# The first shift and scale columns loaded in two pieces, the token root of the latent stream summed on TensorE

## The chip, the cores and the metric

The kernel runs on one core of a Trainium2 chip. The metric is the device time of one execution in microseconds (us). Several executions are timed, and one execution is also recorded by the hardware profiler; its trace gives the rows below.

## What is computed

One layer of a diffusion backbone, in float32, for 512 latent tokens (`x`) and 256 context tokens (`ctx`) of width 2048. The part that matters here is its head:

```python
mod = c_act @ w_mod + b_mod            # 2048 x 12288; sh1 and sc1 are its first 2 x 2048 columns
h  = rmsnorm(x,   g_norm1) * (1 + sc1)  + sh1
hc = rmsnorm(ctx, g_norm1) * (1 + csc1) + csh1
z  = h @ w_in                          # the same for hc; split into heads: q, k (128 each), v (256), ...
```

`rmsnorm` divides each token by the root of the mean square over its 2048 channels. After that come scans over four GLA and four mLSTM heads, an output projection, a gated residual, a second norm, a convolutional MLP and a last norm.

## The kernel before

Activations lie transposed: a channel tile is 128 channels on the partitions by 512 tokens (`xl[k]`, k from 0 to 15, 256 KB each) or by 256 context tokens (`xc[k]`, loaded in pairs). Every large matmul is done as three passes on operands split into a rounded part and a remainder (`hTh`, `hTl` for the stream, `hi_h`, `lo_h` for the weights): ScalarE casts the first, VectorE subtracts to get the second (`split`, lines 89 and 90).

`project_first` is the stage that the diff touches. It projects head 0 (weights `w0`, sums in six PSUM banks, `project_chunk`) and head 1 (weights `w1`, `early_group`, whose partial sums are evicted to SBUF) while the shift and scale columns are still being made. It walks over eight pairs of channel tiles (`kp`). For every pair it needs, in this order:

- the shift (region 0) and scale (region 1) columns of the two tiles. `mod_load` fetches 4 pieces of 512 KB of `w_mod1` for 256 columns of one region, `mod_rows` multiplies them on TensorE with the activated conditions (16 products of 128x32 by 128x256), ScalarE copies the rows out, and `mod_cols` turns them into columns with two small products, from which VectorE makes `scol` or `shcol`;
- `modulate`: a multiplication by the token root, a multiply and add with scale and shift, then the split;
- six groups (`g`): q, k, two pairs of token blocks of v, and two blocks of context tokens.

The token root (`stream_rstd`) is made by squares on ScalarE, a running sum `tot` on VectorE over 16 tiles, a product with a matrix of ones that lays the sum on all partitions, and six operations on 128x512 tiles. The context's root is made in the same way from 8 tiles.

In `project_first` all matmuls are pinned: TensorE runs them in the order of the program text. `tc.high_priority()` moves other engines' work ahead in the order that the scheduler writes out. `tc.issue_after(ins)` queues what its block issues on the engine of `ins` (VectorE here) behind `ins`. All loads go through the queue of SyncE, in program order as the trace shows them; a load into a pool's buffer waits there until the buffer's last reader is done. The pool `mraw` holds four pieces, `wraw` four (weights, and every fourth piece of `w_mod1`), `whi` and `wlo` two each; PSUM has two buffers for the small work (`psb`).

Of the kernel before, what the change touches and what calls it, by code (L numbers as in the profile page):

```python
# [11 lines left out]
F32 = mybir.dt.float32  # L12
F32R = mybir.dt.float32r
U8 = mybir.dt.uint8
AF = mybir.ActivationFunctionType
# [3 lines left out]
P = 128  # L19
D = 2048  # L20
KT = D // P
KP = KT // 2
T = 512
TJ = T // P
# [19 lines left out]
C_SA = C_SEG + T  # L44
C_ONE = C_SA + 32
# [24 lines left out]
def block_kernel(ctx: ExitStack, tc: tile.TileContext, a: dict, out: bass.AP):  # L70
    nc = tc.nc
    V, S, G, PE = nc.vector, nc.scalar, nc.gpsimd, nc.tensor

    def pool(stack, name, bufs=1, space=None, waits="pool"):
        if space is None:
            return stack.enter_context(tc.tile_pool(name=name, bufs=bufs, reuse_waits=waits))
        return stack.enter_context(tc.tile_pool(name=name, bufs=bufs, space=space))
# [128 lines left out]
    def mod_load(region, n):  # L206

        raws = []
        for q in range(4):
            raws.append((wraw if q == 3 else mraw).tile([P, 4, 256], F32, name=f"raw_m{region}_{n}_{q}", tag="raw"))  # L210
            nc.sync.dma_start(raws[q], a["w_mod1"][8 * region + n, q])
        return raws

    def mod_rows(region, n, raws):

        bank = psb(f"ps_m{region}_{n}")
        ps = bank[:, 0:256]
# [4 lines left out]
        rows = tmp.tile([P, 256], F32, name=f"rows_m{region}_{n}", tag="rows")  # L222
        with tc.high_priority():
            S.copy(rows, ps)
        return bank, rows

    def mod_cols(region, n, bank, rows):

        pc = bank[:, 256:260].rearrange("p (b c) -> p b c", c=2)
        for b in range(2):  # L230
            mm(pc[:, b, :], rows[:, P * b : P * b + P], cc(C_SA, 2), start=True, stop=True)
        with tc.high_priority():
            for b in range(2):
                k = 2 * n + b
# [49 lines left out]
        return accp.tile([P, T], F32, name=f"sum{i}_{name}", tag=f"sum{i}")  # L284


    def project_chunk(kp, wh, wl, o, g, first=0, last=KT - 1):

        ks = list(enumerate((2 * kp, 2 * kp + 1)))
        if g < 2:  # L290
            c = slice(P * g, P * g + P)
            for kk, k in ks:
                mm3(o, wh[:, kk, c], wl[:, kk, c], hx[0][k], hx[1][k], k == first, k == last)
        elif g < 4:
            for b in range(2):
                js = slice(P * (2 * g - 4 + b), P * (2 * g - 3 + b))
                for kk, k in ks:
                    mm3(o[:, b, :], hx[0][k][:, js], hx[1][k][:, js], wh[:, kk, 256:], wl[:, kk, 256:],
                        k == first and b == 0, k == last, skip_group_check=True)
        else:  # L300
            js = slice(P * (g - 4), P * (g - 3))
            for kk, k in ks:
                mm3(o, hc[0][k][:, js], hc[1][k][:, js], wh[:, kk, P:], wl[:, kk, P:], k == first, k == last)
# [27 lines left out]
    def project_first():  # L331

        banks = [acc(f"a0_{g}", BANKS[g]) for g in range(6)]
        sums = [None] * 4 + [accp.tile([P, DK + DV], F32, name=f"e0_{4 + j}", tag=f"sum{j}") for j in range(CJ)]
        stream_rstd(xl, rl, "l", T)
        for r in (1, 0):
            mod_cols(r, 0, *mod_rows(r, 0, mod_load(r, 0)))
        w1, w0 = (load_split(a["w_heads"][h, 0], f"h{h}_0") for h in (1, 0))
        for j in range(KT // 2):
            nc.sync.dma_start(xcp[j], a["ctxT"][j])  # L340
        raws = {r: mod_load(r, 1) for r in (1, 0)}
        with tc.high_priority():
            ins = modulate(0, "x")
        for g in range(4):
            early_group(0, g, w1, sums)
        project_chunk(0, *w0, banks[0], 0)
        rows = mod_rows(1, 1, raws[1])
        project_chunk(0, *w0, banks[1], 1)
        mod_cols(1, 1, *rows)
        with tc.high_priority(), tc.issue_after(ins):  # L350
            stream_rstd([x.rearrange("p a b -> p (a b)") for x in xcp], rc, "c", TC)
            ins = modulate(0, "c")
        for g in range(2, 4):
            project_chunk(0, *w0, banks[g], g)
        rows = mod_rows(0, 1, raws[0])
        early_group(0, 4, w1, sums)
        mod_cols(0, 1, *rows)
        early_group(0, 5, w1, sums)
        with tc.issue_after(ins):
            modulate(1, "xc")  # L360
        w1 = load_split(a["w_heads"][1, 1], f"h1_1")
        for r in (1, 0):
            raws[r] = mod_load(r, 2)
        nc.sync.dma_start(cst[:, 0:C_SA], a["consts"][:, 0:C_SA])
# [3 lines left out]
        mod_cols(1, 2, *rows)  # L368
        for kp in range(1, KP):
            for g in range(6):  # L370
                if g == 5 and kp + 1 < KP:
                    rows = mod_rows(0, kp + 1, raws[0])
                ins = early_group(kp, g, w1, sums)
                if g == 2:
                    with tc.issue_after(ins):
                        w0 = load_split(a["w_heads"][0, kp], f"h0_{kp}")
                    if kp + 2 < KP:
                        raws[1] = mod_load(1, kp + 2)
            if kp + 1 < KP:
                mod_cols(0, kp + 1, *rows)  # L380
                with tc.issue_after(ins):
                    modulate(kp + 1, "xc")
            for g in range(6):
                if g == 3 and kp + 2 < KP:
                    rows = mod_rows(1, kp + 2, raws[1])
                project_chunk(kp, *w0, banks[g], g)
                if g == 2 and kp + 1 < KP:
                    w1 = load_split(a["w_heads"][1, kp + 1], f"h1_{kp + 1}")
                    if kp + 2 < KP:
                        raws[0] = mod_load(0, kp + 2)  # L390
                if g == 3 and kp + 2 < KP:
                    mod_cols(1, kp + 2, *rows)
        return banks, sums


# [31 lines left out]

    nc.sync.dma_start(cv, a["cvec"])
    nc.sync.dma_start(cst[:, C_SA:], a["consts"][:, C_SA:])
    nc.sync.dma_start(cols, a["cols"])  # L430
    xl = [ytile(k, f"xl{k}") for k in range(KT)]
    xcp = [actp.tile([P, 2, TC], F32, name=f"xc{j}", tag=f"al{KT // 2 + j}") for j in range(KT // 2)]
# [14 lines left out]
    def stream_rstd(xs, o, name, n):  # L447

        tot = xp.tile([P, T], F32, name=f"sq_{name}", tag="sqs")
        for k, x in enumerate(xs):  # L450
            sq = tot if k == 0 else tmp.tile([P, T], F32, name=f"sq_{name}{k}", tag="sq")
# [6 lines left out]
        var = tmp.tile([P, n], F32, name=f"var_{name}", tag="sq")  # L458
        scr = tmp.tile([P, n], F32, name=f"scr_{name}", tag="sq")
        mean_eps(var, ps, D)  # L460
        rsqrt(var, scr, o)

    rl, rc = rstd[:, 0:T], rstd[:, T:]

    def modulate(n, streams):
        for k in (2 * n, 2 * n + 1):
            if "x" in streams:
                mul(xl[k], xl[k], rl)
            if "c" in streams:
                mul(xc[k], xc[k], rc)  # L470
        for k in (2 * n, 2 * n + 1):
# [656 lines left out]
def arrange(x, c, ctx, c_ctx, w_mod, b_mod, g_norm1, g_norm2, w_in, gla_w_lr, gla_b_lr, mlstm_b_gate,  # L1128
# [10 lines left out]
    r = {}  # L1139
# [7 lines left out]
    r["w_mod1"] = w_mod[0][:, : 2 * D].reshape(4, 4, P, 16, 256).transpose(3, 0, 2, 1, 4)  # L1147
# [42 lines left out]
```

## Time and profile before

| | |
|---|---|
| median of 3 timed runs | 2608.57 us (2608.11 to 2610.57) |
| profiled execution | 2605.73 us, of it the traced span 2604.0 us |
| TensorE busy in the span | 2540.7 us (98%) |
| VectorE, ScalarE, GpSimd busy | 1354.1, 873.3, 230.2 us |
| moved by DMA | 321.39 MB, 123 GB/s over the span |

In the rows below PE is TensorE's matmuls, PEld its weight loads, DVE VectorE, ACT ScalarE, SPq SyncE's queue, which issues the loads. A float32 product of `mm` appears as two MATMUL records. PEclk is the clock granted to TensorE, 1.00 for 2.4 GHz and 0.50 for 1.2 GHz.

### The profile page before, as it was taken

Reading aid. Unit: us, or ns where it says so; the run is one execution under the profiler, and the core shown is the slowest. Engines: PE = TensorE matmul, PEld = TensorE weight load, DVE = VectorE, ACT = ScalarE, POOL = GpSimd, SP = SyncE. Lnnn points to the kernel's source line nnn. Section 1 sums busy time; section 2 is a strip of 40 time slices with the busy share of each in tenths; the row PEclk is TensorE's granted clock in tenths of the full one; section 3 lists DMA queues with packets and bytes.
Section 4 is the critical chain, followed back from the end, with each engine's and each line's share of the span. In section 5 each row is a group of like instructions: output and inputs, shape, how many; then the busy total and the mean of one; then the engine's idle time right before and its main releaser. Section 6 shows DMA issues by size and latency. Waiting matters only on the chain.

```text
span 2604.0 us, 31932 instructions
## 1 busy us (share of the span) xinstructions
PE 2540.7 (98%) x12866; PEld 2132.3 (82%) x12866; DVE 1354.1 (52%) x1969; ACT 873.3 (34%) x1289; POOL 230.2 (9%) x183
## 2 busy tenths in 40 slices
PE   5999999999999999999999999999999999999998
PEld 4887888888897878878878888888888888888887
DVE  6566765553344455448576336533653365336534
ACT  4224543332324344334443123312331233123332
POOL 0000000111212223210331000000000000000001
PEclk9999999999999999999999999999999999999999
DMA  8851112222333576642654322333333223322333
GB/s 312 291 194 42 33 41 74 73 79 84 122 122 122 191 227 220 201 140 85 213 182 146 97 97 98 97 97 97 97 96 97 96 95 96 98 96 90 100 97 101
DMA packets 96349, 321.39 MB, mean 123 GB/s; under 512 B 10884, under 2 KB 15304, under 8 KB 96200
## 3 DMA queue, kind: packets, MB, share of 16 engines
q1 hardware_dynamic: 96200, 319.34, 37.4%
q8 instruction: 101, 1.65, 0.3%
q14 instruction: 48, 0.39, 0.0%
HBM read 315.10 MB, written 4.19 MB: 123 GB/s over the span
## 4 chain that ended last, share of the span: by engine, by line
PE 87%; DVE 4%; DMA 4%; ACT 2%; issue 2%; POOL 1%; SPq 0%; POOLq 0%; ACTq 0%; DVEq 0%
PE a L95 18%; PE dn L95 17%; PE ug L95 17%; PE uv L95 17%; PE wo L95 6%; DMA raw_m<-in_w_mod 4%; PE ga L95 4%; PE po L95 3%; PE ps_m L95 1%; PE sl L95 1%; DVE cv L1037 1%; PE dl L95 1%; POOL sum_m L257 1%; PE cst L95 0%; PE s L95 0%
## 5 line engine op out<-in xcount | busy, mean ns | idle before, releaser
L95 PE MATMUL ug<-h2h,hi_ug 128*128 128x512 f32 x688 | 269.0, 392 | 1.6 <-ACT h2h L996 1.6
L95 PE MATMUL uv<-h2h,lo_uv 128*128 128x512 f32 x688 | 267.9, 389 | 1.5 <-DVE lo_uv L90 1.5
L95 PE MATMUL ug<-h2h,lo_ug 128*128 128x512 f32 x688 | 268.7, 390 | 0.1
L95 PE MATMUL ug<-h2l,hi_ug 128*128 128x512 f32 x688 | 268.4, 390 | 0.0
L95 PE MATMUL uv<-h2h,hi_uv 128*128 128x512 f32 x688 | 267.9, 389 | 0.5 <-ACT hi_uv L89 0.5
L95 PE MATMUL uv<-h2l,hi_uv 128*128 128x512 f32 x688 | 267.7, 389 | 0.0
L95 PE MATMUL dn<-gh,hi_d 128*128 128x512 f32 x644 | 250.5, 389 | 0.0
L95 PE MATMUL dn<-gl,hi_d 128*128 128x512 f32 x644 | 250.5, 389 | 0.0
L95 PE MATMUL dn<-gh,lo_d 128*128 128x512 f32 x644 | 250.5, 389 | 0.0
L1037 DVE SCALAR_TENSOR_TENSOR cv<-pad,cwt,cv 128x512 f32<-128x512 f32 x344 | 242.3, 759 | 10.6 <-ACT cv L1035 9.1
L90 DVE TENSOR_TENSOR lo_ug<-raw_ug,hi_ug 128x1024 fp32r<-128x1024 f32 (+1 forms) x88 | 107.4, 1220 | 238.7 <-ACT hi_ug L89 238.6
L257 POOL TENSOR_TENSOR sum_m<-sum_m,raw_m 128x512 f32<-128x512 f32 x112 | 177.8, 1588 | 577.1 <-ACT raw_m L256 360.3
L90 DVE TENSOR_TENSOR lo_uv<-raw_uv,hi_uv 128x1024 fp32r<-128x1024 f32 (+1 forms) x88 | 105.4, 1198 | 182.1 <-ACT hi_uv L89 181.6
L90 DVE TENSOR_TENSOR lo_d<-raw_d,hi_d 128x1024 fp32r<-128x1024 f32 x82 | 98.7, 1203 | 165.5 <-ACT hi_d L89 164.6
L89 ACT CAST hi_ug<-raw_ug 128x1024 fp32r<-128x1024 f32 (+1 forms) x88 | 90.8, 1032 | 262.4 <-PE ug L95 194.7
L89 ACT CAST hi_d<-raw_d 128x1024 fp32r<-128x1024 f32 x82 | 85.1, 1037 | 278.7 <-PE dn L95 224.4
L255 DVE SCALAR_TENSOR_TENSOR sum_m<-raw_m,csil,sum_m 128x512 f32<-128x512 f32 x112 | 95.0, 849 | 158.4 <-DMA raw_m<-in_w_mod 158.0
L89 ACT CAST hi_uv<-raw_uv 128x1024 fp32r<-128x1024 f32 (+1 forms) x88 | 90.9, 1033 | 250.5 <-PE uv L95 181.1
L95 PEld LDWEIGHTS ug<-h2h,hi_ug 128*128 128x128 f32 x688 | 129.8, 189 | 28.7 <-ACT h2h L996 1.9
L95 PEld LDWEIGHTS uv<-h2h,lo_uv 128*128 128x128 f32 x688 | 129.1, 188 | 29.3 <-DVE lo_uv L90 2.4
L95 PEld LDWEIGHTS ug<-h2h,lo_ug 128*128 128x128 f32 x688 | 129.6, 188 | 28.2 <-DVE lo_ug L90 1.0
L95 PEld LDWEIGHTS ug<-h2l,hi_ug 128*128 128x128 f32 x688 | 129.7, 189 | 27.0
(302 smaller groups left out, 5218.5 us busy)
## 6 DMA issues: line engine op xcount, KB each, us to landing
raw_m<-in_w_mod SPq DMA_DIRECT2D x192, 512.0 KB, 4.3
raw_ug<-in_w_up SPq DMA_DIRECT2D x80, 512.0 KB, 3.4
raw_uv<-in_w_up SPq DMA_DIRECT2D x80, 512.0 KB, 3.3
raw_d<-in_w_down SPq DMA_DIRECT2D x79, 512.0 KB, 3.5
raw_h<-in_w_heads SPq DMA_DIRECT2D x64, 512.0 KB, 3.4
raw_ga<-in_w_gates SPq DMA_DIRECT2D x32, 512.0 KB, 4.3
raw_wo<-in_w_out SPq DMA_DIRECT2D x32, 512.0 KB, 4.3
xl<-in_xT SPq DMA_DIRECT2D x16, 256.0 KB, 5.1
```

Source lines behind the costliest of these rows:

```text
L89: S.copy(hi, x)
L90: return V.tensor_tensor(out=lo, in0=x, in1=hi.bitcast(F32), op=ALU.subtract).ins
L95: ins = PE.matmul(*args, **kw)
L255: V.scalar_tensor_tensor(out=dv, in0=raw[:, 0, :], scalar=ce, in1=dv, op0=ALU.mult, op1=ALU.add)
L257: G.tensor_tensor(out=po, in0=po, in1=raw[:, 1, :], op=ALU.add)
L1037: V.scalar_tensor_tensor(out=t3, in0=src, scalar=w, in1=t3, op0=ALU.mult, op1=ALU.add)
```

## The change

The first two pieces of shift and scale columns (256 columns of each region) are loaded as two times 128 columns from an own array `w_mod0` (two loads of 512 KB for each piece). The products and columns are made for one channel tile at a time, and head 0 begins with channel tile 0 alone (`only=0`), then tile 1. Head 1's first groups follow behind them. The latent stream's squares are added in pairs on VectorE and summed over channels on TensorE into four columns (tokens on partitions); the root is worked out on 128x4 tiles, and four products with the identity lay it on all partitions again (`rb`). The first two tiles are multiplied by `rb` before their columns are there (`scaled`); ScalarE copies `rb` to `rl` for the others. The identity's 64 KB are loaded ahead of `xl` instead of later with the other constants. The weights `w0` are loaded before the first pieces, `w1` between them. `mraw` has six buffers.

```diff
-        stream_rstd(xl, rl, "l", T)
-        for r in (1, 0):
-            mod_cols(r, 0, *mod_rows(r, 0, mod_load(r, 0)))
-        w1, w0 = (load_split(a["w_heads"][h, 0], f"h{h}_0") for h in (1, 0))
+        ss = psb("ss_l", (P, TJ))
+        for k in range(0, KT, 2):
+            sqs = [tmp.tile([P, T], F32, name=f"sq_l{k + i}", tag=f"sq{i}") for i in range(2)]
+            for i in range(2):
+                S.activation(sqs[i], xl[k + i], AF.Square)
+            if k < KT - 2:
+                add(sqs[0], sqs[0], sqs[1])
+                del sqs[1]
+            for i, sq in enumerate(sqs):
+                for j in range(TJ):
+                    mm(ss[:, j : j + 1], sq[:, P * j : P * j + P], cst[:, C_ONE : C_ONE + 1], ...)
+        w0 = load_split(a["w_heads"][0, 0], "h0_0")
+        halves = [{r: mod_load_half(r, 0) for r in (1, 0)}]
+        w1 = load_split(a["w_heads"][1, 0], "h1_0")
+        halves.append({r: mod_load_half(r, 1) for r in (1, 0)})
         for j in range(KT // 2):
             nc.sync.dma_start(xcp[j], a["ctxT"][j])
         raws = {r: mod_load(r, 1) for r in (1, 0)}
+        rows = mod_rows(1, 0, halves[0][1], P)
+        var, scr, r = (xp.tile([P, TJ], F32, name=f"{n}_l") for n in ("var", "scr", "rs"))
         with tc.high_priority():
-            ins = modulate(0, "x")
+            mean_eps(var, ss, D)
+            rsqrt(var, scr, r)
+        rb = psb("rb_l")
+        for j in range(TJ):
+            mm(rb[:, P * j : P * j + P], r[:, j : j + 1].to_broadcast([P, P]), ident, start=True, stop=True)
+        mod_cols(1, 0, *rows, 1)
+        rows = mod_rows(0, 0, halves[0][0], P)
+        mod_cols(0, 0, *rows, 1)
+        with tc.high_priority():
+            for k in range(2):
+                mul(xl[k], xl[k], rb)
+            S.copy(rl, rb)
+            ins = modulate((0,), "x", True)
         for g in range(4):
-            early_group(0, g, w1, sums)
-        project_chunk(0, *w0, banks[0], 0)
-        rows = mod_rows(1, 1, raws[1])
-        project_chunk(0, *w0, banks[1], 1)
-        mod_cols(1, 1, *rows)
+            project_chunk(0, *w0, banks[g], g, only=0)
+        for r in (1, 0):
+            mod_cols(r, 1, *mod_rows(r, "0b", halves[1][r], P), 1)
+        with tc.high_priority():
+            ins = modulate((1,), "x", True)
+        for g in range(4):
+            project_chunk(0, *w0, banks[g], g, only=1)
         with tc.high_priority(), tc.issue_after(ins):
             stream_rstd([x.rearrange("p a b -> p (a b)") for x in xcp], rc, "c", TC)
-            ins = modulate(0, "c")
-        for g in range(2, 4):
-            project_chunk(0, *w0, banks[g], g)
+            ins = modulate((0, 1), "c")
+        for g in range(3):
+            early_group(0, g, w1, sums)
+        rows = mod_rows(1, 1, raws[1])
+        early_group(0, 3, w1, sums)
+        mod_cols(1, 2, *rows)
+        early_group(0, 4, w1, sums)
         rows = mod_rows(0, 1, raws[0])
-        early_group(0, 4, w1, sums)
-        mod_cols(0, 1, *rows)
         early_group(0, 5, w1, sums)
+        mod_cols(0, 2, *rows)
         with tc.issue_after(ins):
-            modulate(1, "xc")
+            modulate((2, 3), "xc")
...
-    mraw = pool(st_0, "mraw", 4)
+    mraw = pool(st_0, "mraw", 6)
```

Behind this, in both kernels: `load_split` of head 1's second pair, `mod_load` for the third pair, `project_chunk(4)`, `mod_rows(1, 2)`, `project_chunk(5)`, `mod_cols`, and then the loop over `kp` from 1 to 7, which is the same but for the numbering of the columns.

## Rows read from the trace of the kernel before

**Rows 1.** The page: busy time, share of the span and instructions of each engine.
```profile
PE 2540.7 (98%) x12866; PEld 2132.3 (82%) x12866; DVE 1354.1 (52%) x1969; ACT 873.3 (34%) x1289; POOL 230.2 (9%) x183
```

**Rows 2.** Windows of 10 us: busy time by engine, PEclk, DMA share, GB/s.
```profile
0.00:10.00 10.00, 0.00 (x0) 0.00 (x0) 4.95 (x12) 5.27 (x8) 0.20 (x4) 1.00 0.71 228
10.00:20.00 10.00, 1.21 (x2) 0.50 (x2) 7.62 (x11) 6.30 (x10) 0.00 (x0) 1.00 1.04 411
20.00:30.00 10.00, 5.96 (x62) 2.20 (x60) 4.78 (x9) 1.63 (x3) 0.00 (x0) 0.97 0.75 270
...
50.00:60.00 10.00, 9.64 (x97) 7.18 (x95) 8.61 (x21) 4.78 (x11) 0.00 (x0) 1.00 0.88 320
60.00:70.00 10.00, 9.50 (x72) 8.15 (x76) 5.66 (x12) 0.94 (x4) 0.00 (x0) 1.00 0.89 323
...
80.00:90.00 10.00, 10.00 (x65) 9.27 (x63) 5.47 (x9) 2.10 (x4) 0.00 (x0) 1.00 0.91 352
```

**Rows 3.** The chain of waits from 0 to 150 us: start, us, what.
```profile
18.79 2.07 PE ss_l L95 x2
...
23.17 6.79 DMA raw_m<-in_w_mod
...
35.75 8.85 PE a L95 x41
...
62.75 6.79 PE a L95 x42
69.55 1.86 PE ps_m L95 x32
71.41 1.26 PE a L95 x6
72.67 0.34 PE ps_m L95 x4
73.00 4.30 PE a L95 x24
```

**Rows 4.** Timeline, 2 to 35 us: start, us, instruction, what ended the idle time before.
```profile
2.18 8.57 SPq L435 DMA_DIRECT2D xl<-in_xT  x16
...
8.48 10.25 DVE L86 TENSOR_TENSOR sq_l<-sq_l,sq_l 128x512 f32<-128x512 f32 x13 [0.62 <-ACT sq_l L452]
...
20.79 2.79 PE L95 MATMUL ps_m<-raw_m,cact 128*32 128x256 f32 x32
...
30.01 1.08 PE L95 MATMUL ps_m<-raw_m,cact 128*32 128x256 f32 x8 [0.60 <-DMA raw_m<-in_w_mod]
...
32.70 0.34 DVE L239 TENSOR_SCALAR shcol<-ps_m,cols 128x2 f32<-128x2 f32 x2 [5.51 <-PE ps_m L95]
...
34.21 0.80 PE L95 MATMUL a<-hTh,hi_h 128*128 128x512 f32 x1 [1.62 <-ACT hTh L89]
```

**Rows 5.** Waits of the load queue from 13 to 15 us: us, times, longest.
```profile
SPq L211 <- DMA xl<-in_xT: 0.6, 2, 0.3
```

**Rows 6.** Timeline of the second norm's token root, which is made in column form.
```profile
1163.36 2.39 PE L968 MATMUL ps_rms<-cst,sqsq 128*128 128x1 f32 x20 [0.76 <-ACT sqsq L956]
...
1165.79 0.16 DVE L154 TENSOR_SCALAR rs_rms<-ps_rms 128x4 f32<-128x4 f32 x1 [1.76 <-PE ps_rms L968]
...
1167.36 2.05 PE L975 MATMUL rb_rms<-cst,rs_rms 128*128 128x128 f32 x8 [1.61 <-DVE rs_rms L83]
```

**Rows 7.** Timeline of TensorE in its first projection: two products in a row.
```profile
37.20 0.63 PE L95 MATMUL a<-hTl,hi_h 128*128 128x512 f32 x1
...
37.62 0.63 PE L95 MATMUL a<-hTh,lo_h 128*128 128x512 f32 x1
```

**Rows 8.** Groups by line, 20 to 95 us: count, busy us, mean ns, idle before.
```profile
L86 DVE TENSOR_TENSOR sq_c<-sq_c,sq_c 128x512 f32<-128x512 f32 x7 | 4.8, 692 | 2.4 <-ACT sq_c L452 2.0
L452 ACT ACTIVATE sq_c<-xc 128x512 f32<-128x512 f32 x8 | 4.7, 624 | 0.0
```

**Rows 9.** Timeline of TensorE: the sum for the context's root, and a later wait.
```profile
48.24 1.11 PE L95 MATMUL ss_c<-sq_c,cst 128*128 128x256 f32 x4
...
60.50 0.64 PE L95 MATMUL ps_m<-raw_m,cact 128*32 128x256 f32 x8 [0.61 <-DMA raw_m<-in_w_mod]
```

**Rows 10.** Windows around the second norm's token root.
```profile
1165.00:1167.00 2.00, 0.75 (x7) 0.66 (x6) 0.64 (x4) 0.41 (x2) 0.00 (x0) 0.76 0.80 262
1167.00:1171.00 4.00, 2.05 (x8) 1.78 (x8) 1.46 (x4) 0.83 (x2) 0.00 (x0) 0.50 0.00 0
1171.00:1176.00 5.00, 4.96 (x12) 3.90 (x13) 4.88 (x9) 2.32 (x3) 0.00 (x0) 0.50 0.00 0
```

**Rows 11.** Loads by line, 0 to 75 us: count, KB each, median us to landing.
```profile
raw_m<-in_w_mod SPq DMA_DIRECT2D x29, 512.0 KB, 6.6
```

More of the change, by code (lines that the diff above doesn't have):

```diff
@@ L210, in mod_load, with mod_load_half, mod_rows @@
             raws.append((wraw if q == 3 else mraw).tile([P, 4, 256], F32, name=f"raw_m{region}_{n}_{q}", tag="raw"))
-            nc.sync.dma_start(raws[q], a["w_mod1"][8 * region + n, q])
+            nc.sync.dma_start(raws[q], a["w_mod1"][7 * region + n - 1, q])
         return raws
-    def mod_rows(region, n, raws):
+    def mod_load_half(region, b):
+        raws = []
+        for i in range(2):
+            pl = wraw if region == 0 and b == 1 else mraw
+            raw = pl.tile([P, 2, 4, P], F32, name=f"raw_mh{region}_{b}_{i}", tag="raw")
+            nc.sync.dma_start(raw, a["w_mod0"][region, b, i])
+            raws += [raw[:, 0], raw[:, 1]]
+        return raws
+    def mod_rows(region, n, raws, w=256):
         bank = psb(f"ps_m{region}_{n}")
-        ps = bank[:, 0:256]
+        ps = bank[:, 0:w]
         for q in range(4):
@@ L221, in mod_rows @@
                    start=(q == 0), stop=(q == 3), skip_group_check=True)
-        rows = tmp.tile([P, 256], F32, name=f"rows_m{region}_{n}", tag="rows")
+        rows = tmp.tile([P, w], F32, name=f"rows_m{region}_{n}", tag="rows")
         with tc.high_priority():
@@ L225, in mod_rows, with mod_cols @@
         return bank, rows
-    def mod_cols(region, n, bank, rows):
-        pc = bank[:, 256:260].rearrange("p (b c) -> p b c", c=2)
-        for b in range(2):
+    def mod_cols(region, k0, bank, rows, nb=2):
+        pc = bank[:, 256 : 256 + 2 * nb].rearrange("p (b c) -> p b c", c=2)
+        for b in range(nb):
             mm(pc[:, b, :], rows[:, P * b : P * b + P], cc(C_SA, 2), start=True, stop=True)
         with tc.high_priority():
-            for b in range(2):
-                k = 2 * n + b
+            for b in range(nb):
+                k = k0 + b
                 if region == 1:
@@ L284, in sum_tile, with project_chunk @@
         return accp.tile([P, T], F32, name=f"sum{i}_{name}", tag=f"sum{i}")
-    def project_chunk(kp, wh, wl, o, g, first=0, last=KT - 1):
-        ks = list(enumerate((2 * kp, 2 * kp + 1)))
+    def project_chunk(kp, wh, wl, o, g, first=0, last=KT - 1, only=None):
+        ks = [(kk, k) for kk, k in enumerate((2 * kp, 2 * kp + 1)) if only in (None, kk)]
         if g < 2:
@@ L334, in project_first @@
         sums = [None] * 4 + [accp.tile([P, DK + DV], F32, name=f"e0_{4 + j}", tag=f"sum{j}") for j in range(CJ)]
-        stream_rstd(xl, rl, "l", T)
-        for r in (1, 0):
-            mod_cols(r, 0, *mod_rows(r, 0, mod_load(r, 0)))
-        w1, w0 = (load_split(a["w_heads"][h, 0], f"h{h}_0") for h in (1, 0))
+        ss = psb("ss_l", (P, TJ))
+        for k in range(0, KT, 2):
+            sqs = [tmp.tile([P, T], F32, name=f"sq_l{k + i}", tag=f"sq{i}") for i in range(2)]
+            for i in range(2):
+                S.activation(sqs[i], xl[k + i], AF.Square)
[4 more added lines that the diff above has]
+                for j in range(TJ):
+                    mm(ss[:, j : j + 1], sq[:, P * j : P * j + P], cst[:, C_ONE : C_ONE + 1],
+                       start=(k == 0 and j == 0), stop=(k == KT - 2 and i == 1), skip_group_check=True)
+        w0 = load_split(a["w_heads"][0, 0], "h0_0")
+        halves = [{r: mod_load_half(r, 0) for r in (1, 0)}]
+        w1 = load_split(a["w_heads"][1, 0], "h1_0")
+        halves.append({r: mod_load_half(r, 1) for r in (1, 0)})
         for j in range(KT // 2):
@@ L363, in project_first @@
             raws[r] = mod_load(r, 2)
-        nc.sync.dma_start(cst[:, 0:C_SA], a["consts"][:, 0:C_SA])
+        nc.sync.dma_start(cst[:, P:C_SA], a["consts"][:, P:C_SA])
         project_chunk(0, *w0, banks[4], 4)
@@ L367, in project_first @@
         project_chunk(0, *w0, banks[5], 5)
-        mod_cols(1, 2, *rows)
+        mod_cols(1, 4, *rows)
         for kp in range(1, KP):
@@ L379, in project_first @@
             if kp + 1 < KP:
-                mod_cols(0, kp + 1, *rows)
+                mod_cols(0, 2 * kp + 2, *rows)
                 with tc.issue_after(ins):
-                    modulate(kp + 1, "xc")
+                    modulate((2 * kp + 2, 2 * kp + 3), "xc")
             for g in range(6):
@@ L391, in project_first @@
                 if g == 3 and kp + 2 < KP:
-                    mod_cols(1, kp + 2, *rows)
+                    mod_cols(1, 2 * kp + 4, *rows)
         return banks, sums
@@ L429, in block_kernel @@
     nc.sync.dma_start(cst[:, C_SA:], a["consts"][:, C_SA:])
+    nc.sync.dma_start(cst[:, 0:P], a["consts"][:, 0:P])
     nc.sync.dma_start(cols, a["cols"])
@@ L450, in stream_rstd @@
         for k, x in enumerate(xs):
-            sq = tot if k == 0 else tmp.tile([P, T], F32, name=f"sq_{name}{k}", tag="sq")
+            sq = tot if k == 0 else tmp.tile([P, T], F32, name=f"sq_{name}{k}", tag="sq0")
             S.activation(sq, x, AF.Square)
@@ L457, in stream_rstd @@
             mm(ps, ones, tot[:, i : i + n], start=(i == 0), stop=(i + n == T))
-        var = tmp.tile([P, n], F32, name=f"var_{name}", tag="sq")
-        scr = tmp.tile([P, n], F32, name=f"scr_{name}", tag="sq")
+        var = tmp.tile([P, n], F32, name=f"var_{name}", tag="sq0")
+        scr = tmp.tile([P, n], F32, name=f"scr_{name}", tag="sq1")
         mean_eps(var, ps, D)
@@ L463, in block_kernel, with modulate @@
     rl, rc = rstd[:, 0:T], rstd[:, T:]
-    def modulate(n, streams):
-        for k in (2 * n, 2 * n + 1):
-            if "x" in streams:
+    def modulate(ks, streams, scaled=False):
+        for k in ks:
+            if "x" in streams and not scaled:
                 mul(xl[k], xl[k], rl)
@@ L470, in modulate @@
                 mul(xc[k], xc[k], rc)
-        for k in (2 * n, 2 * n + 1):
+        for k in ks:
             if "x" in streams:
@@ L1146, in arrange @@
     r["ctxT"] = ctx[0].T.reshape(KT // 2, 2, P, TC).transpose(0, 2, 1, 3)
-    r["w_mod1"] = w_mod[0][:, : 2 * D].reshape(4, 4, P, 16, 256).transpose(3, 0, 2, 1, 4)
+    m = w_mod[0][:, : 2 * D].reshape(4, 4, P, 2, D)
+    r["w_mod0"] = m[..., : 2 * P].reshape(2, 2, 4, P, 2, 2, P).transpose(4, 5, 0, 3, 1, 2, 6)
+    r["w_mod1"] = m[..., 2 * P :].reshape(4, 4, P, 14, 256).transpose(3, 0, 2, 1, 4)
     r["w_mod2"] = w_mod[0][:, 2 * D :].reshape(KP, 2, P, 4, 4, 512).transpose(3, 4, 0, 2, 1, 5)
```

## The prediction

> **What bounds the kernel now.** The page comes first: TensorE is busy in 98% of the span [rows 1], so a change can only give what TensorE stands still or runs slowly. The windows say where that is: none of its work before 18.8 us, 5.96 of 10 us between 20 and 30, and from 50 to 70 us only 0.36 and 0.50 us are missing; at 80 to 90 nothing is [rows 2]. The chain of waits tells why: the running sum of the squares on VectorE (13 additions stretch over 10.25 us), the sum for the root at 18.79, a piece of columns that lands at 29.96, and then TensorE's own work from 34.21 on [rows 3, 4]. The loop over the pairs starts with the group at 62.75 [rows 3]; from there I found no wait of TensorE for the rest of the stage. So the whole gain is what the start of that loop moves forward, and what comes behind it moves with it. I follow the changed program to that start.
>
> **The loads.** The rate is 228 GB/s up to 10 us and 411 after it [rows 2]. The latent stream is 4.19 MB, the constants 0.11 MB; 2.28 MB are there at 10 us and the rest at 10 + 2.02 / 0.411 = 14.9 us. I allow 0.8 us from the last byte to the signal: the queue still waits for `xl` between 13 and 15 us [rows 5]. The identity, now ahead, costs one issue, 8.57 / 16 = 0.5 us [rows 4], and 0.15 us of bytes: the stream is in at 15.5, signalled at 16.3. With six buffers and no earlier reader nothing holds the queue until the second pieces are reused, so every 512 KB take 0.524 / 0.411 = 1.28 us: `w0`, then the first scale half (two loads) signalled at 20.1, the first shift half at 22.7, `w1`, the second halves at 26.5 and 29.1, the context at 34.2, the two next pieces (four loads each) at 39.3 and 44.4.
>
> **The token root.** Removed are 16 serial additions and six operations on 128x512. The squares now run at the pace of the loads; the last is done at 16.3 + 0.6. Products for sums of columns took 2.39 us for 20 records, 0.12 each [rows 6]; the last two squares make 16 records, 1.9 us from 16.4, so 18.3. The root in column form took 1.57 us from its first operation to the first product that lays it out [rows 6]: 19.9 us. So the root is ready before the scale half (20.1), and the root is no longer what is late; the loads are.
>
> **To the first product.** TensorE keeps the program's order: the rest of the scale rows (0.7 us), the four products that lay the root out, 2.05 us [rows 6], the column and its scale 0.8, the shift rows. A set of rows 256 wide takes 1.86 us [rows 3] or 2.79 in the start [rows 4]. At 128 wide no row shows it: from half of 1.86, if columns count, to all of it, if the number of instructions does; I take 1.4 as the middle. That gives 20.1 + 0.7 + 2.05 + 0.8 + 1.4 = 25.05. From the end of the last rows to the first product it was 34.21 - 31.09 = 3.1 us [rows 4]; with half a row copy and one column instead of two I take 2.4. Head 0 starts at 27.4 instead of 34.2: 6.8 us earlier.
>
> **What that is worth.** Tile 0 gives only half the work: four groups, a half of 4.30 + 1.5, 2.9 us at the full clock [rows 3]; at the lower level products come every 0.42 us [rows 7], 12 of 512 columns make 5.1. With 0.7 us until the remainder `hTl` is there it ends at 30.8 or 32.8. Then nothing is left for TensorE but the second halves: twice 1.4 for rows and 0.7 for copy and column, 4.2 us, and 1.5 from the shift column to the next product [rows 4], since that product needs it: tile 1 begins at 36.5 or 38.5. In the old order four groups of head 1 and more covered such chains.
>
> The step that takes the gain back is the context's root. Its additions are queued on VectorE behind the last subtraction of tile 1 (37.2 or 39.2), and its product on TensorE now stands ahead of every group of head 1. Seven additions take 4.8 us of work [rows 8]; chained with squares through two buffers they come every 10.25 / 13 = 0.79 us [rows 4], 5.5 us. The squares (8 of 0.62) hide in that. TensorE has only tile 1's four groups meanwhile, 2.9 to 5.1 us, and stands until 42.7 or 44.7. The product takes 1.1 [rows 9]: 43.8 or 45.8. Queued behind it are all six groups of head 1 (8.05 us), two of head 0 on the context (2.3), three sets of rows (5.6) and three of columns (1.0), from the chain's rows 6.79 + 1.26, 1.86 and 0.34 [rows 3]: 17.0 us. The loop starts at 60.8 or 62.8, against 62.75. What hides in these 17 us: the context's own root and split (about 5 us, needed after 9), the next pieces (in at 44.4, needed at 48 and 53), and the weights. The gain is 0 to 2 us; I take 1.0, the middle. The half-wide rows move it by up to 1 either way.
>
> Sum: span 2604.0 - 1.0, with the 1.7 us that lie around the span 2604.7 for the profiled execution (2605.73). The median shown is 2608.57, 2.8 above that execution, so the predicted median is 2607.6.
>
> **The rivals.** *The clock is high from the start.* If the sums, rows and layout products bring TensorE to 2.4 GHz before 20 us, its own steps halve and only loads set the start: first product about 25.6, tile 1 at 31.8 behind the half signalled at 29.1, additions from 32.5, product done at 39.1, loop at 56.1: 6.6 us gained, 2602.0. For it: the granted clock reads 0.97 between 20 and 30 us [rows 2]. Against it: the set of rows there took 2.79 us and not 1.86 [rows 3, 4], and in the second norm's root, 20 such column sums did not keep the level, it stood at 0.50 behind them [rows 10]. Chance 0.15, 0.12 of it above the bound below.
>
> *The clock falls in each gap.* Around that root the granted clock was 0.50 from 1167 to 1176, 5 us of it in dense products behind a gap in TensorE's work [rows 10]. The changed start has such gaps before tile 0, before tile 1 and at the context's product; the first two only fill the wait, the third would cost half of 5 us: loop at 62.8 + 2.5, 2.5 us lost, 2611.1. Chance 0.14. The Trainium skill, TensorE: Matmul & The Clock Gate, section "HAM oscillation — how this bites in real kernels", says that a kernel whose bursts of matmuls wait for data in between starts burst after burst at half rate; by that rule this rival would be the result, and rows 10 agree with it for one gap.
>
> *Slower by a load.* With six buffers the third scale piece waits for the set of rows before it, done at about 50 to 52, and is needed at 57.3 to 59.3. A piece lands 6.6 us after its issue [rows 11], so about 1 us is spare; in the old kernel this same product waited 0.61 us [rows 9]. If landing takes 8 us or more, TensorE waits here instead; at 13 us the loop starts at 68.5 and the time is 2614. Chance 0.05.
>
> *It starts no earlier.* If the halves come at the 270 GB/s of 20 to 30 us [rows 2] and VectorE's split of `w1` stands ahead of the first column, the first product is back near 33 to 34, with the serial chain behind it: loop at 67 to 69, 2614.5. Against it: the 270 came from a queue that waited for buffers, which now are free. Chance 0.05.
>
> **Numbers.** The forecast's own case (gain 0 to 2, with the rows' bounds -1 to 3) has 0.61: 2605.6 to 2609.6. About 0.2% of the time, 5.2 us, is what a measurement of this kernel tells from no change. Faster by more: 0.12, from the first rival. Slower by more: 0.08, from the two last, which do not all pass the bound. The rest is 0.80. The range takes in most of the two clock rivals and a run's own spread of 1 to 2 us: 2602.5 to 2611.5.
>
> **What would show it.** Right: first projection product near 27 us; VectorE's `sq_c` additions directly behind the second `hTl`; TensorE waiting for them by 2 to 4 us ahead of `ss_c` at about 44; then 17 us without a break to the loop near 62. Wrong: `ss_c` before 40, no wait ahead of it, or a granted clock of 1.00 from 20 us on (the gain would be 5 us or more); a wait for `raw_m` ahead of the third scale rows, or a first product after 31 us (a loss).

## The result

The changed kernel takes 2613.39 us (median of 22 runs, 2609.95 to 2621.87), the kernel before 2607.53 us (22 runs, 2603.19 to 2613.80): ratio 1.0022, interval 1.0015 to 1.0028, so 5.9 us slower. The forecast was 2607.6 us with a range of 2602.5 to 2611.5 and a chance of 0.08 for slower: wrong. The profiled execution has a span of 2612.0 us, 8.0 more than before.

The timeline of the changed kernel (start, us, instruction) from the column sums to the loop over the pairs, with VectorE's additions for the context:

```profile
19.42 5.28 PE L95 MATMUL ss_l<-cst,sq_l 128*128 128x1 f32 x24 [0.20 <-DVE sq_l L86]
...
24.63 1.93 PE L95 MATMUL ps_m<-raw_mh,cact 128*32 128x128 f32 x32
...
26.49 2.08 PE L95 MATMUL rb_l<-cst,rs_l 128*128 128x128 f32 x8
...
32.93 0.80 PE L95 MATMUL a<-hTh,hi_h 128*128 128x512 f32 x1 [1.54 <-ACT hTh L89]
...
44.36 0.50 PE L95 MATMUL a<-hTh,hi_h 128*128 128x512 f32 x1 [1.54 <-ACT hTh L89]
...
44.95 5.39 DVE L86 TENSOR_TENSOR sq_c<-sq_c,sq_c 128x512 f32<-128x512 f32 x7
...
50.48 1.10 PE L95 MATMUL ss_c<-sq_c,cst 128*128 128x256 f32 x4 [1.09 <-DVE sq_c L86]
```

The chain of waits of the changed kernel from 50 us on, and TensorE's last wait ahead of the loop:

```profile
50.48 1.10 PE ss_c L95 x4
51.59 4.19 PE a L95 x24
...
70.80 6.79 PE a L95 x42
...
81.05 4.30 PE a L95 x24
```

```profile
70.19 0.61 PE L95 MATMUL ps_m<-cst,rows_m 128*128 128x2 f32 x4 [1.18 <-ACT rows_m L234]
```

Windows of 10 us of the changed kernel (busy time by engine, PEclk, DMA share, GB/s):

```profile
10.00:20.00 10.00, 9.41 (x43) 9.15 (x42) 3.46 (x5) 6.31 (x12) 0.00 (x0) 1.00 1.04 411
20.00:30.00 10.00, 9.25 (x81) 8.67 (x84) 3.44 (x9) 2.02 (x5) 0.00 (x0) 1.00 1.03 415
30.00:40.00 10.00, 7.78 (x76) 6.11 (x68) 2.58 (x5) 2.35 (x4) 0.00 (x0) 0.66 0.96 382
40.00:50.00 10.00, 6.74 (x62) 5.27 (x54) 6.15 (x11) 5.88 (x11) 0.00 (x0) 0.83 0.60 214
```

The loop starts with the group of 42 records at 70.80, against 62.75 before [rows 3]: 8.05 us later, and the span is longer by 8.0. In these two traces all of the loss lies ahead of the loop; that the two numbers agree so closely is partly chance, since in the other traces below the shift of the loop and that of the span differ by 0.1 to 9.5 us. TensorE shows more busy time in the first 30 us than before [rows 2], but this is the column sums: 24 records from 19.42 take 5.28 us, one starts every 0.21 us (a record lasts 0.35 us and overlaps the next). Loads are not what it waits for: they run at 411 and 415 GB/s from 10 to 30 us without a break. The first projection product comes at 32.93, only 1.3 us earlier than before [rows 4].

Below, an experiment's loop start is read in the same way from its chain, from one trace for each kernel. Where the program is the same, such stretches repeat well: from the group behind the context's product to the loop it is 19.2 us in the changed kernel and in four of the experiments. But the moment at which TensorE's clock falls can differ between two traces whose programs are equal up to there, which is worth 1 to 2 us (see the dense products in the gaps), so differences of that size are weak evidence. Behind the stage the profiled executions differ by several microseconds among themselves, and the interval of a ratio over ten runs is 2 to 3 us to either side.

| kernel | first product | loop starts | ratio to before (95%) |
|---|---|---|---|
| before | 34.21 | 62.75 | 1 |
| changed | 32.93 | 70.80 | 1.0022 (1.0015 to 1.0028) |
| changed, old root | 28.97 | 66.36 | 1.0007 (0.9996 to 1.0017) |
| before, column root alone | 38.27 | 66.78 | 1.0003 (0.9993 to 1.0014) |
| changed, sums of four tiles | 29.66 | 67.78 | 1.0006 (0.9995 to 1.0018) |
| the same, dense products between | 31.39 | 69.80 | 1.0014 (1.0004 to 1.0024) |
| changed, context's sum later | 32.73 | 69.34 | 1.0027 (1.0016 to 1.0039) |
| before, six buffers alone | 30.24 | 57.55 | 0.9981 (0.9969 to 0.9994) |
| changed, columns of tile 1 early | 35.26 | 63.44 | 1.0010 (0.9999 to 1.0021) |
| changed, all three repairs | 34.32 | 62.40 | 0.9986 (0.9977 to 0.9995) |
| six buffers, dense products ahead | 29.61 | 57.08 | 0.9977 (0.9964 to 0.9989) |
| the same, column root from one sum | 33.07 | 61.76 | 0.9994 (0.9985 to 1.0003) |
| the same with old root, dense in gaps | 31.11 | 58.61 | 0.9985 (0.9976 to 0.9994) |
| changed, four buffers | 32.26 | 72.27 | 1.0044 (1.0030 to 1.0057) |

### The profile page after: what moved, and what is told of

Read it like the earlier page. It is cut to its first block, busy times and chain, and to the rows that moved or that the text cites. A ratio compares the mean times of both kernels' runs of the same rounds, so it can differ in the third digit from the quotient of the medians.

```text
span 2612.0 us, 32213 instructions
## 1 busy us (share of the span) xinstructions
PE 2559.7 (98%) x13008; PEld 2155.8 (83%) x13008; DVE 1353.0 (52%) x1961; ACT 873.9 (33%) x1292; POOL 229.5 (9%) x183
## 3 DMA queue, kind: packets, MB, share of 16 engines
HBM read 315.10 MB, written 4.19 MB: 122 GB/s over the span
## 4 chain that ended last, share of the span: by engine, by line
PE 90%; DVE 4%; DMA 2%; issue 2%; ACT 1%; POOL 0%; SPq 0%; POOLq 0%; DVEq 0%; ACTq 0%
PE a L95 18%; PE ug L95 17%; PE dn L95 17%; PE uv L95 17%; PE wo L95 6%; PE ga L95 6%; PE po L95 3%; PE ps_m L95 1%; PE sl L95 1%; DMA raw_m<-in_w_mod 1%; DVE cv L1079 1%; PE dl L95 1%; PE s L95 0%; PE cst L95 0%; PE mc L276 0%
## 5 line engine op out<-in xcount | busy, mean ns | idle before, releaser
L265 DVE SCALAR_TENSOR_TENSOR sum_m<-raw_m,csil,sum_m 128x512 f32<-128x512 f32 x112 | 101.6, 908 | 146.0 <-DMA raw_m<-in_w_mod 145.8
L95 PEld LDWEIGHTS uv<-h2h,hi_uv 128*128 128x128 f32 x688 | 129.1, 188 | 28.6 <-ACT hi_uv L89 1.9
```

The costliest lines, as they stand in the source:

```text
L95: ins = PE.matmul(*args, **kw)
L265: V.scalar_tensor_tensor(out=dv, in0=raw[:, 0, :], scalar=ce, in1=dv, op0=ALU.mult, op1=ALU.add)
```

## The experiments

**The old root in the changed kernel.**

```diff
-        (column sums of the squares, root on 128x4, layout by four products)
+        stream_rstd(xl, rl, "l", T)
...
-            ins = modulate((0,), "x", True)
+            ins = modulate((0,), "x")
```

> The changed kernel with the token root of the latent stream made as before: running sum on VectorE, product with the matrix of ones, root on 128x512. Theory A (the column sums, 0.23 us each in the start, hold the root until 24.7 us and with it everything behind): the running sum ends near 19.2, the root near 26.3, the first projection product comes near 28.3 instead of 32.9, and the loop over the pairs starts near 66.2 instead of 70.8: 4.6 us less than the changed kernel, about 1.001 of the kernel before. Theory B (the serial chain of tile 1 and the context's root ahead of head 1 end on something that the start does not move, a load or VectorE): the first product moves, the loop still starts at 70 to 71, 1.002 of before.

The timeline of TensorE in this kernel:

```profile
19.30 2.08 PE L95 MATMUL ss_l<-sq_l,cst 128*128 128x512 f32 x2 [19.30 <-DVE sq_l L86]
21.30 1.94 PE L95 MATMUL ps_m<-raw_mh,cact 128*32 128x128 f32 x32
...
28.97 0.79 PE L95 MATMUL a<-hTh,hi_h 128*128 128x512 f32 x1 [3.07 <-ACT hTh L89]
```

The start of the loop in its chain of waits:

```profile
66.36 6.78 PE a L95 x42
```

The first product moves by 4.0 us and the loop by 4.4. What moves the start moves the stage: theory B, that the rest ends on something else, falls. The root in column form costs 4.4 us here, and 3.6 us of the loss against before stay.

**The column root alone in the kernel before.** Four buffers, whole pieces and the old order.

```diff
-        stream_rstd(xl, rl, "l", T)
+        (column sums of the squares, root on 128x4, layout by four products)
```

> The kernel before with one part of the change alone: the column sums on TensorE, the root on 128x4, its layout by four products, the identity loaded early. Pieces, order and four buffers as before. Theory A: the sums end near 24.7, so the rows of the first scale piece start 3.9 us later than before, the buffers for the last shift pieces come free that much later, the first product is near 37.5 instead of 34.2, and the time is 3 to 4 us longer than before, 1.0013. Theory B (the order is to blame and the root costs nothing): first product within 1 us of 34.2, the time the same.

The loop starts 4.0 us later, at 66.78, and the first product 4.1 us later: theory A. The median does not tell this from no change (interval 0.9993 to 1.0014; 1.0013 was expected).

**Sums of four tiles.**

```diff
-        for k in range(0, KT, 2):
+        for k in range(0, KT, 4):      # VectorE adds four squares, TensorE sums the result
```

> The changed kernel, but VectorE adds the squares of four tiles before TensorE sums them over channels: 32 column-sum records instead of 72, and no square waits for TensorE. Theory A: sums end near 19.8, the layout of the root near 24.2 instead of 28.6, the first product near 28.3, the loop near 66.2: 4 to 5 us less than the changed kernel, 1.001 of before. Theory B: the loop still starts at 70 to 71. If the sums cost 0.12 each here, they end near 18.9 and the first product near 27.5.

The timeline of TensorE in this kernel:

```profile
15.38 1.87 PE L95 MATMUL ss_l<-cst,sq_l 128*128 128x1 f32 x8 [0.71 <-DVE sq_l L86]
18.22 1.86 PE L95 MATMUL ss_l<-cst,sq_l 128*128 128x1 f32 x8 [0.97 <-DVE sq_l L86]
...
22.20 2.04 PE L95 MATMUL rb_l<-cst,rs_l 128*128 128x128 f32 x8 [0.25 <-PE ps_m L95]
```

The price shows once more, 1.86 us for 8 records, and the sums are done at 20.1 (19.8 expected). The layout is done 4.3 us earlier, but the loop gains 3.0, not 4.6: the shift rows, which ran at the full clock in the changed kernel (1.08 us for 32 records), took 1.94 here. So the sums were moved, and the clock took a part of it back.

**Dense products between the sums**, in the kernel with the sums of four tiles:

```diff
+        dense(4)                       # 128x128 by 128x512, zeros, result not used
         for k in range(0, KT, 4):
...
+            if k < KT - 4:
+                dense(1)
```

> The sums-of-four kernel with extra dense products on TensorE whose results are not used: four products of 128x128 by 128x512 on a tile of zeros ahead of the first column sums, one behind each of the first three sets. Theory A, in the form that the column sums, the rows and the first projection are slow by the clock (0.23, 0.06 and 0.43 us a record there, about half later): sums at 0.12 each, the last set ends near 19.2 instead of 20.1, the layout takes 1.0 instead of 2.0, the first product comes near 27.5 instead of 29.7, tile 0's products take 2.9 instead of 5.0, the loop starts near 63.5 instead of 67.8. If the slowness is of the instructions themselves and not of the clock: all as in the sums-of-four kernel, loop at 67.8 or later by what the extra products take.

Windows of this kernel:

```profile
8.00:10.00 2.00, 0.00 (x0) 0.00 (x0) 1.33 (x2) 1.85 (x4) 0.00 (x0) 1.00 1.04 395
10.00:12.00 2.00, 1.90 (x9) 1.80 (x10) 1.37 (x3) 1.87 (x4) 0.00 (x0) 0.65 1.04 392
12.00:16.00 4.00, 4.00 (x12) 2.50 (x11) 2.83 (x5) 3.36 (x6) 0.00 (x0) 0.50 1.06 412
16.00:20.00 4.00, 4.00 (x12) 2.55 (x11) 2.08 (x3) 2.36 (x4) 0.00 (x0) 0.50 1.02 418
```

A miss of the setup: behind the first burst TensorE stood from 8 to 10 us, the granted clock fell to 0.50 (1.2 of 2.4 GHz) between 10 and 12 us, and single dense products between the sums did not bring it back. The loop came 2.0 us later than with the sums of four alone. It shows the sums at 0.21 us from start to start (8 in 1.71 us) at a granted clock of 0.50. The first set, in which the clock falls, took 1.46 us: its first records start 0.11 us apart, its last 0.21.

**Six buffers and a closed row of dense products.** A second attempt at the clock, with the old root:

```diff
-    mraw = pool(st_0, "mraw", 4)
+    mraw = pool(st_0, "mraw", 6)
...
+        for _ in range(14):            # zeros, result not used
+            mm(banks[0], dm[:, 0:P], dm, start=True, stop=True)
         stream_rstd(xl, rl, "l", T)
```

> The kernel before with six buffers and 14 dense products on zeros, not used, on TensorE ahead of the sum for the root, where it is idle. Theory A in its clock form: they end near 18, the sum for the root takes 1.0 instead of 2.1 us, the scale rows 1.9 instead of 3.6, the first projection comes near 29 instead of 30.2 and its first 41 records take 6.5 instead of 8.5; the loop starts near 54.5 instead of 57.55: 3 us less than six buffers alone, 0.997 of before. If the clock is not the cause: the dense products run late and the loop starts at 57.5 or later.

The timeline of TensorE in this kernel:

```profile
1.38 15.17 PE L95 MATMUL a<-dm 128*128 128x512 f32 x28 [1.38 <-POOL dm L336]
19.20 1.12 PE L95 MATMUL ss_l<-sq_l,cst 128*128 128x512 f32 x2 [2.65 <-DVE sq_l L86]
20.25 1.93 PE L95 MATMUL ps_m<-raw_m,cact 128*32 128x256 f32 x32
```

The root's sum takes 1.12 us instead of 2.07 [rows 3], the scale rows 1.93 instead of 3.64 without the dense products. So work ahead of them sets their speed. The loop gains only 0.5 us: the first product then waits for the shift pieces, and the projection's first 41 records still take 8.6 us, since the clock fell again between 27 and 28 us.

**The column sums behind dense products.** The kernel with the closed row of dense products, but with the column root, from a single running sum:

```diff
-        stream_rstd(xl, rl, "l", T)
+        (running sum on VectorE; 8 column-sum records; root on 128x4; layout)
```

> Six buffers and dense products as in the run before, and the token root in column form from one running sum: 8 column-sum records behind 14 dense products. If the clock makes the sums slow (0.23 in the changed kernel, 0.21 at a granted clock of 0.50 in the sums-of-four run with dense products), they take 0.12 each here, 1.0 us for 8, and the layout 1.0 to 1.2 instead of 2.0. If the instruction itself is slow in this place, 1.9 and 2.0. The loop starts within 1 us of 57.1 either way, since the first product waits for the shift pieces at 26.

The timeline of TensorE in this kernel:

```profile
1.38 14.89 PE L95 MATMUL a<-dm 128*128 128x512 f32 x28 [1.38 <-POOL dm L336]
19.47 1.13 PE L95 MATMUL ss_l<-cst,sq_l 128*128 128x1 f32 x8 [3.21 <-DVE sq_l L86]
20.54 3.48 PE L95 MATMUL ps_m<-raw_m,cact 128*32 128x256 f32 x32
23.94 1.16 PE L95 MATMUL rb_l<-cst,rs_l 128*128 128x128 f32 x8
```

Eight column sums take 1.13 us, one starts every 0.11 us, against 0.21 without dense work ahead. The same instruction, at two speeds, and again at 0.21 where the granted clock reads 0.50 (dense products between the sums): the clock is the cause. The expected loop start was missed by 4.7 us; the clock fell right behind the sums (granted 0.66 on average from 19 to 23 us), the rows there ran at half rate, 3.48 us, and the first product came at 33.1, so this is no better version.

**Six buffers alone.**

```diff
-    mraw = pool(st_0, "mraw", 4)
+    mraw = pool(st_0, "mraw", 6)
```

> The kernel before with six buffers in the pool of the pieces instead of four, nothing else. Theory A (the start is late because of what its first product waits for): the shift pieces no longer wait for the scale rows, the last of them lands near 26.5 instead of 30.0, the first product comes near 30.7 instead of 34.2, TensorE is busy from there to the loop, which starts near 59.5 instead of 62.75: 3 us less than before, 0.9987. Theory B (what comes behind ends on loads): the loop stays within 1 us of 62.75, the time the same.

The load queue before:

```profile
11.12 12.47 SPq L211 DMA_DIRECT2D raw_m<-in_w_mod  x8
```

The load queue and TensorE in this kernel, and the start of the loop in its chain:

```profile
11.10 4.83 SPq L211 DMA_DIRECT2D raw_m<-in_w_mod  x8
...
20.92 3.64 PE L95 MATMUL ps_m<-raw_m,cact 128*32 128x256 f32 x32
25.59 1.93 PE L95 MATMUL ps_m<-raw_m,cact 128*32 128x256 f32 x32
...
30.24 0.50 PE L95 MATMUL a<-hTh,hi_h 128*128 128x512 f32 x1 [1.62 <-ACT hTh L89]
```

```profile
57.55 6.79 PE a L95 x42
```

The eight pieces are issued in 4.8 us instead of 12.5, the first product comes 4.0 us earlier and the loop 5.2. The time falls to 2602.27 us, ratio 0.9981. This one line of the change is worth more than expected (3 us); the rest of the change, put on top of it, costs 13.25 us of the stage (57.55 to 70.80).

**Four buffers in the changed kernel.**

```diff
-    mraw = pool(st_0, "mraw", 6)
+    mraw = pool(st_0, "mraw", 4)
```

> The changed kernel with four buffers instead of six, nothing else. If the buffers are worth in this order what they are in the old one (5.2 us): loop near 76. By the order of the loads here: the second scale half waits for the scale rows at 24.7 to 26.6, lands by 32 and is needed at 39, so the first product and tile 1 stay; the pieces for pair 1 wait for buffers until 40 and until the third scale rows at 55.7, which makes the shift rows near 61 wait some 3 us: loop at 73 to 75.

The timeline of TensorE in this kernel, the end of the scale rows of the third pair:

```profile
67.05 0.64 PE L95 MATMUL ps_m<-raw_m,cact 128*32 128x256 f32 x8 [1.18 <-DMA raw_m<-in_w_mod]
68.64 1.08 PE L95 MATMUL ps_m<-raw_m,cact 128*32 128x256 f32 x8 [0.94 <-DMA raw_m<-in_w_mod]
```

The loop starts 1.5 us later, at 72.27, with TensorE waiting 1.18 and 0.94 us for the last pieces of the third pair's scale rows (not for the shift rows near 61, as the expectation said). In this order the start hardly needs the extra buffers: the first product comes at 32.26, no later than with six.

**Tile 1's columns ahead of tile 0's products.**

```diff
+        for r in (1, 0):
+            mod_cols(r, 1, *mod_rows(r, "0b", halves[1][r], P), 1)
         for g in range(4):
             project_chunk(0, *w0, banks[g], g, only=0)
-        for r in (1, 0):
-            mod_cols(r, 1, *mod_rows(r, "0b", halves[1][r], P), 1)
```

> The changed kernel with the rows and columns of channel tile 1 made ahead of tile 0's products instead of behind them. Theory C (what the first product does not explain, some 9 us between the changed kernel with the old root and the old order with six buffers, is the serial chain of tile 1, for which TensorE has nothing to do): first product 33 to 34.5, tile 1's products directly behind tile 0's, the context's product near 43.5 instead of 50.5, loop near 64 instead of 70.8. Theory B (loads or VectorE end the stage): loop at 69 or later.

The chain of waits of this kernel:

```profile
43.14 1.10 PE ss_c L95 x4
...
63.44 6.79 PE a L95 x42
```

The context's product comes at 43.14 instead of 50.48 and the loop 7.4 us earlier, as theory C expected, although the first product comes 2.3 us later (35.26). Tile 0's products, 5.06 us at half rate in the changed kernel, no longer stand ahead of tile 1's columns, and here they ran at full rate. The serial chain between the two tiles is the largest loss of the new order among the parts that were tried.

**The context's sum behind the first group of head 1.**

```diff
-        with tc.high_priority(), tc.issue_after(ins):
-            stream_rstd([... for x in xcp], rc, "c", TC)
-            ins = modulate((0, 1), "c")
-        for g in range(3):
+        early_group(0, 0, w1, sums)
+        with tc.high_priority(), tc.issue_after(ins):
+            stream_rstd([... for x in xcp], rc, "c", TC)
+            ins = modulate((0, 1), "c")
+        for g in range(1, 3):
             early_group(0, g, w1, sums)
```

> The changed kernel with the context's root traced behind the first group of head 1 instead of ahead of it, so that its product no longer stands ahead of that group on TensorE; VectorE's additions stay where they are. Theory A (the place of the context's product costs only the gap in front of it, 1.1 us, the start costs the rest): group 0 fills the gap, the loop starts near 69.6 instead of 70.8. Theory B (the place of the context's product is the main loss): the loop starts 3 us or more earlier, at 67.5 or before.

The timeline of TensorE in this kernel, its last product ahead of the loop:

```profile
68.73 0.61 PE L95 MATMUL ps_m<-cst,rows_m 128*128 128x2 f32 x4 [1.18 <-ACT rows_m L234]
```

Its windows, for the first stretch of the loop:

```profile
70.00:72.00 2.00, 2.00 (x6) 1.58 (x5) 0.02 (x1) 0.26 (x1) 0.00 (x0) 0.50 1.03 416
```

The loop starts 1.5 us earlier, a little more than the gap of 1.09. But its first 42 records then take 8.35 us instead of 6.79, at a granted clock of 0.50 between 70 and 72 us, and at the next mark (81.14 against 81.05) nothing is left of it. The place of the context's product is not the main loss.

**The three repairs together**, sums of four tiles, early columns, the context's sum later:

> The changed kernel with the three repairs together: sums of four tiles, tile 1's columns ahead of tile 0's products, the context's root behind the first group of head 1. Theory A and C together: 3.0 from the sums, 7.4 from the columns, about 1.3 from the context's place, counted from 70.8: the loop starts near 59, some 3.5 us earlier than before, 0.9985 of it, and no better than six buffers alone (57.55): then the half pieces and the new order add nothing to the buffers. If the half pieces have a worth of their own, the loop starts before 57.

The loop starts at 62.40, not 59: the repairs don't add up. With four sets of rows in a row at half rate (1.93 us each, and about 0.4 of waiting for each copy) the first product is back at 34.32. Against six buffers alone (57.55) the half pieces and the new order add nothing. The median is below before's (0.9986), more than the stage's 0.35 us explain; the rest lies behind the stage and is not explained.

**Dense products in the gaps**, a try at a better version:

```diff
-        for r in (1, 0):
-            mod_cols(r, 0, *mod_rows(r, 0, mod_load(r, 0)))
+        mod_cols(1, 0, *mod_rows(1, 0, mod_load(1, 0)))
+        (two dense products)
+        mod_cols(0, 0, *mod_rows(0, 0, mod_load(0, 0)))
+        (one dense product)
```

> The six-buffer kernel with 14 dense products ahead of the root's sum, two more between the scale columns and the shift rows and one behind the shift columns. If the clock fell in the gaps from 23 to 31 us because TensorE had little to do there, the first 41 records of the projection take 6.5 instead of 8.6 us and the loop starts near 55.5 (57.1 without). If they do not hold the clock: 57.5 or later.

The timeline of TensorE in this kernel, the scale rows and the first projection products:

```profile
19.02 1.12 PE L95 MATMUL ss_l<-sq_l,cst 128*128 128x512 f32 x2 [2.80 <-DVE sq_l L86]
20.07 3.55 PE L95 MATMUL ps_m<-raw_m,cact 128*32 128x256 f32 x32
...
33.69 0.47 PE L95 MATMUL a<-hTh,lo_h 128*128 128x512 f32 x1
33.95 0.63 PE L95 MATMUL a<-hTh,hi_h 128*128 128x512 f32 x1
34.38 0.63 PE L95 MATMUL a<-hTl,hi_h 128*128 128x512 f32 x1
```

A miss: the projection begins at full speed and falls to a product every 0.43 us from its seventh on. The loop starts at 58.61, 1.5 us later than without. The comparison is not clean: up to the scale rows the two kernels are the same, but here the clock fell behind the root's sum and these rows took 3.55 us instead of 1.93.

Four versions have an interval that lies below 1 against the kernel before: six buffers alone (0.9981, 2602.27 us), with dense products ahead (0.9977, 2600.51 us), with dense products in the gaps (0.9985) and the three repairs together (0.9986). The gains are 0.14 to 0.23% and their intervals overlap, so no run shows that anything is better than the one line.

## Why the prediction was wrong

- *What bounds the kernel, and that the gain is what the loop's start moves forward.* Right in these two traces: the loop moved by 8.05 us, the profiled span by 8.0. The median moved by 5.9.
- *The loads.* Right: 411 and 415 GB/s in the windows, no break, and TensorE waits for no load in the start.
- *The token root.* This is the step that failed: "0.12 each [rows 6]; the last two squares make 16 records, 1.9 us from 16.4, so 18.3", and from it "the root is no longer what is late; the loads are". The sums measured 0.22 to 0.23 us each by the same count (24 in 5.28, 16 in 3.64), and 72 of them in a row took from 7.9 to 24.7 us. The squares also waited for TensorE to free their buffers (six times, 4.6 us). The sums ended 6.4 us later than forecast. The rows that I took the price from stand behind dense work at the full clock (TensorE busy for all of 1150 to 1160 us, granted clock 1.00); here nothing dense stands ahead. The run behind 14 dense products has the sums of [rows 6] again, one every 0.11 us, so the size was wrong by the clock and not the instruction. The layout's 2.05 us came from the same group of rows, but from a stretch at a granted clock of 0.50 [rows 10], and it was right: 2.08.
- *To the first product.* 32.9 instead of 27.4. By the trace 4.5 of the 5.5 us are the sums, which end at 24.6 where the forecast goes on at 20.1, and 1.2 the scale rows, which all stand behind the sums and ran at half rate (1.93 instead of 0.7). With sums of four tiles the first product came 3.3 us earlier, with the old root 4.0. Half-wide rows were taken at 1.4 us between bounds; they measured 1.93 at half rate and 1.08 at full rate, half of what whole ones take (3.64 and 1.93).
- *The serial chain of tile 1.* Right in kind and nearly in size: from the first product to tile 1's first it took 11.4 us (forecast 9.1 to 11.1). Moving the columns ahead gave 7.4 us back.
- *The context's root takes the gain back.* The additions took 5.39 us (forecast 5.5) and its product ended 7.2 us behind tile 1's start (forecast 7.3). But TensorE stood only 1.1 us, not 2 to 4, since tile 1's products ran at half rate meanwhile. As a cause it is small: filling the gap gave 1.5 us, and this was lost again.
- *17.0 us without a break to the loop.* It took 19.2 (51.59 to 70.80). Two waits that were not foreseen: 0.35 for an eviction and 1.18 for a copy of rows. By the timeline the copy stands on ScalarE behind a cast that waits for VectorE; this was argued from the trace and not tried.
- *The sum.* The forecast's late end was 62.8. Add 5.5 for the start, 0.3 for the chain, 2.2 for the last stretch: 70.8, as measured. This only says where the forecast and the trace part. With the old root in place of the failed step the loop still starts at 66.36, 3.6 us behind that late end and behind the kernel before: 1.6 of it lies ahead of the first product (28.97) and 2.2 in the last stretch. So the failed step explains 4.4 of the 8.0 us of loss, and not all of it.
- *The rivals.* The clock was not high from the start. That it falls in each gap was half right: tile 0's products (5.06 us on the path, where the forecast has them "only fill the wait") and most of tile 1's ran at half rate, head 1's groups behind the context's product did not (24 records in 4.19 us). The Trainium skill, TensorE: Matmul & The Clock Gate, section "HAM oscillation — how this bites in real kernels", has bursts behind waits start at half rate again. One of the three bursts here agrees: tile 0's products start at half rate, tile 1's start at a product every 0.23 us and fall to 0.43 from the sixth on, and head 1's stay at full rate. No load made the stage slower. "It starts no earlier" was nearest in its result (1.3 us earlier), and wrong in its mechanism.
- *The signs.* A first product after 31 us, named as the sign of a loss, came. A granted clock of 1.00 from 20 us on, named as the sign of a gain, came too, but only as a reading: the sums ran at half rate under it (see the last section). The reading of 0.97 before [rows 2], put down for the first rival, has the same flaw.

What the change is made of, then, in the stage: six buffers alone -5.2 us; half pieces and new order on top of them, with the old root, +8.8 (57.55 to 66.36); the column root +4.4 (to 70.80). In another sequence the parts weigh otherwise: the two buffers are worth 1.5 us in the changed kernel, the column root costs 4.0 in the kernel before. The new order of the loads (`w0` and the identity earlier) was not tried by itself.

## What to carry to other kernels

A price read where an engine runs at full clock is not the price at a program's start: look at what TensorE did just before, and take both levels as the bounds. A unit of work cut in half so that it may start earlier also leaves half as much to cover the next serial chain; count what the engine has left to do until the second half is ready. When several edits come together, try the plainest one alone: two more buffers gave a gain here, and the rest of the change a loss.

## What was not expected of the hardware

TensorE can be busy almost without a break and stay at half rate: in the changed kernel it shows 9.41 of 10 us from 10 to 20, all column sums of 128x128 by 128x1, and at 24 us one still starts every 0.21 us, where 0.11 is the full rate. Fourteen dense products ahead brought it to full rate. In one run it held this over a gap of 2.65 us and until 27 us; in the two others with the same dense products it fell at 20 us, behind gaps of 2.80 and 3.21 us and the sum for the root. Single dense products between sums did not bring it back.

The granted clock in the windows reads 1.00 from the beginning, also where products run at half rate: the same sum for the root took 2.07 us in the kernel before and 1.12 behind dense products, with a reading of 1.00 in both. In these traces the reading can be relied on only once it has changed for the first time; ahead of that the instructions' own durations tell the rate.
